# Differential attention in one float32 product instead of rounded halves

## The chip, the cores and the metric

The kernel runs on one core of a Trainium2 chip. The metric is the device time of one execution in microseconds (us), from start to end; of several executions the median is given. The core has a matrix engine (TensorE, "PE" in the profile, with its weight loads listed apart as "PEld"), a vector engine (VectorE, "DVE"), a scalar engine (ScalarE, "ACT"), a general one (GpSimd, "POOL") and a queue that issues transfers (SyncE, "SP"). Each works through its own list of instructions in a fixed order and waits at semaphores for the others.

## The reference, cut to what matters

One layer of an encoder on 1024 tokens of width 1024: a half-step feed-forward block, then two attention mixers side by side, a gated sum, and a second half-step feed-forward block. The change concerns the second mixer, the differential attention, with 4 heads, two maps of 64 for queries and keys per head, and values of width 128 (128 queries at a time, keys in chunks of 64 up to the query's own):

```python
sc = jnp.einsum('bqhrd,bkhrd->bhrqk', qblk, k).astype(jnp.float32) * scale
...
p = jax.nn.softmax(sc, axis=-1)
attn = p[:, :, 0] - lam * p[:, :, 1]
return jnp.einsum('bhqk,bkhe->bqhe', attn.astype(v.dtype), v)
...
o = rms_norm(o, subln_g) * (1.0 - lambda_init)
```

## The kernel before, in words

Matrix products run on a rounded 32-bit format (float32r) and recover the lost bits by halves: a number is split into its rounded value "hi" and the rest "lo". `split` does this with one ACT cast (line 97) and one DVE subtraction (line 102). A large product is then three products, hi by hi, lo by hi and hi by lo (lines 128 to 130).

The stages follow each other: first feed-forward block; its output projection; the mixer's input projections (queries, keys, gates, and the values by `project_v`, once for each mixer, branch `br` 0 for the band attention "A" and 1 for the differential attention "B"); the attention jobs; the gated output; the second feed-forward block. Projections go to DRAM and come back by `load_qkv` head by head.

`project_v` hands each finished 128x2x256 block to its `sink`. For B it splits two row blocks of 128 tokens into tiles `vo` of 512 columns, in which a head's 128 hi columns stand beside its 128 lo columns, and stores them to DRAM (`v`).

The attention stage runs a list of jobs: 32 for A (4 pairs of heads by 4 double blocks by 2 heads), then 32 for B (4 heads by 8 query blocks of 128). A job is a generator with stages, and `run` interleaves up to five of them, so that one job's scores are computed beside an older one's products. A B job i of a head (i = 0 to 7, key width (i+1)*128):

- scores `sc` (lines 779, 780: `qs` by `ks` and by the exchanged `kl`) for both maps; DVE adds the bias `nb` (787), ACT takes the exponential (789); DVE combines both maps into one `pm` (922 to 927).
- `transpose_p` turns `pm` in blocks of 128 on PE into `pt` (795), up to four blocks a tile, and splits it into `whi` and `wlo` (97, 102).
- for each of the i+1 key blocks two products into `pv`: `whi` by the 256 columns of `vt`, hi and lo (943), and `wlo` by its 128 hi columns (944). That makes 144 blocks over the 32 jobs.
- ACT scales both column halves of `pv` into `o1` and `o2` (946, 948), POOL adds them (949), DVE takes the mean square (952), POOL the power (`r`, 139) and the diagonal tile `dg` (955), PE the product `try` of `o1` and `dg` (958; both operands are plain float32), and ACT and DVE split it into `y` (99, 104).

Beside the jobs, one step of a filler (`branch_a`) is emitted every two B jobs: it loads a gate tile `gl`, makes 12 products `pb` of 512 columns, multiplies them (DVE, 892) and stores them to `ta` (893). Four times it also loads weights `wa`. The weights `raw` of `w_branch_b` and further `gl` come at the end.

The tiles `qs`, `ks`, `kl`, `vt`, `y`, `nb` share one pool of 14 buffers (`big`); `pv` and `pb` share two PSUM buffers. All loads and stores named here are issued by SP in one fixed order. That order, and the order on each engine, is set at build time by a scheduler that works on its own estimate of the times, so a change of one instruction can move others.

Of the kernel before, what the change touches and what calls it, by code (L numbers as in the profile page):

```python
# [54 lines left out]
def hybrid_layer_kernel(ctx, tc, x, ffn1_norm, ffn1_w_in, ffn1_w_out, mix_norm, w_mix_in,  # L55
# [516 lines left out]
    v_d = drams(2, [S, 2 * HALF], "v", F32R)  # L572
# [67 lines left out]
    with tc.tile_pool(name="ps1", bufs=1, space=PSUM) as ps:  # L640
# [24 lines left out]
        def project_v(br, c0):  # L665
# [6 lines left out]
            def make_sink(a):  # L672
                def sink(th, blk, ap):
                    for s in range(2):
                        o = sb.tile([P, HALF], F32R, tag="f", bufs=TF, name="vo")
                        if br == 0:
                            hi = bass.AP(o.tensor, o.offset, [o.ap[0], [256, 2], [192, 2], [1, 64]])
                            lo = bass.AP(o.tensor, o[:, 64:65].offset, [o.ap[0], [256, 2], [64, 2], [1, 64]])
                            src = ap[:, s, :].rearrange("p (a b d) -> p a b d", a=2, b=2)
                        else:  # L680
                            hi, lo = (o.rearrange("p (h c d) -> p h c d", h=2, c=2)[:, :, c, :] for c in range(2))
                            src = ap[:, s, :].rearrange("p (h d) -> p h d", h=2)
                        split(src, hi, lo)
                        t = 4 * th + 2 * a + s
                        move(nc.sync, v_d[br][t * P:(t + 1) * P, blk * HALF:(blk + 1) * HALF], o)
                return sink
# [63 lines left out]
    with tc.tile_pool(name="ps2", bufs=1, space=PSUM) as ps:  # L750
# [6 lines left out]
        def load_qkv(n, parts=1):  # L757
# [8 lines left out]
            vt = big([P, NT, 256], "vt")  # L766
            move(nc.sync, vt, v_d[n // 4].rearrange("(t p) c -> p t c", p=P)[:, :, (n % 4) * 256:(n % 4 + 1) * 256])
            return qs, ks, kl, vt

        def scores(qkv, h, i, k0, w):  # L770

            qs, ks, kl, _ = qkv
# [18 lines left out]
        def transpose_p(blocks):  # L791
# [4 lines left out]
            return split_units(pt[:, :len(blocks), :].rearrange("p b q -> p (b q)"))  # L796
# [22 lines left out]
        def jobs_a(pr):  # L819
            ctx_ = {}  # L820

            def job(sb_, h):
                if not ctx_:
                    ctx_["qkv"] = load_qkv(pr)
                    ctx_["y"] = big([P, 2, S], "y")
# [4 lines left out]
                qkv, y, nb = (ctx_[n] for n in ("qkv", "y", "nb"))  # L830
                vt = qkv[3]
# [65 lines left out]
        def jobs_b(hb, filler):  # L897
            ctx_ = {}

            def job(i):  # L900
                if not ctx_:
# [3 lines left out]
                    if hb % 2 == 0:  # L905
                        nbs.append(big([P, 2, S], "nb", F32))
                        for hh in range(2):
                            bias_rows(nbs[-1][:, hh, :], diag_b, hb + hh, EB, WB)
                    ctx_["nb"] = nbs[-1][:, hb % 2, :]
# [146 lines left out]
```

## Time and profile before

| | before |
|---|---|
| median of 3 executions | 2154.29 us (2150.46 to 2155.05) |
| span of the profiled execution | 2151.1 us |
| PE busy | 2080.7 us (97%) |
| DVE busy | 1442.3 us (67%) |
| ACT busy | 980.2 us (46%) |
| POOL busy | 181.4 us (8%) |
| moved by DMA | 333.55 MB |

For the profiled execution the profile gives the span from its first to its last instruction, and no time beside it. In the profile "busy" counts an instruction from its start to its end; matmuls overlap, and their ends are modelled, so the pace of PE is read from the distance between starts, and not from durations. A group's row gives the number of instructions, their busy time and mean duration in ns, and behind the bar the idle time of the engine just before them with what ended it. PEclk is the granted clock of TensorE as a share of full speed. One 128-column float32 matmul of the program appears as two weight loads and two matmuls in the trace (`try`: 32 in the program, 64 records).

### The profile page before, as it was taken

Reading aid. Unit: us, or ns where it says so; the run is one execution under the profiler, and the core shown is the slowest. Engines: PE = TensorE matmul, PEld = TensorE weight load, DVE = VectorE, ACT = ScalarE, POOL = GpSimd, SP = SyncE. Lnnn points to the kernel's source line nnn. Section 1 sums busy time; section 2 is a strip of 40 time slices with the busy share of each in tenths; the row PEclk is TensorE's granted clock in tenths of the full one; section 3 lists DMA queues with packets and bytes.
Section 4 is the critical chain, followed back from the end, with each engine's and each line's share of the span. In section 5 each row is a group of like instructions: output and inputs, shape, how many; then the busy total and the mean of one; then the engine's idle time right before and its main releaser. Section 6 shows DMA issues by size and latency. Waiting matters only on the chain.

```text
span 2151.1 us, 29100 instructions
## 1 busy us (share of the span) xinstructions
PE 2080.7 (97%) x10073; PEld 1738.7 (81%) x10073; DVE 1442.3 (67%) x2650; ACT 980.2 (46%) x1919; POOL 181.4 (8%) x282
## 2 busy tenths in 40 slices
PE   6999999999999999999999988999999999999997
PEld 5788888888888788899788877788788888888886
DVE  7666566677577756566488977558766656658566
ACT  5433333334446544444498665146433333334444
POOL 2120000000001000000066233001000000000001
PEclk9999999999999999999999999999999999999999
DMA  6653333294445544553683364634543333366334
GB/s 194 173 169 111 95 96 120 93 327 143 117 128 162 168 142 164 198 196 136 230 275 105 136 211 133 233 119 151 172 156 95 111 96 95 114 237 228 98 117 158
DMA packets 277555, 333.55 MB, mean 155 GB/s; under 512 B 15404, under 2 KB 167996, under 8 KB 277408
## 3 DMA queue, kind: packets, MB, share of 16 engines
q1 hardware_dynamic: 276080, 327.94, 46.7%
q0 software_dynamic: 1184, 3.24, 0.6%
q8 instruction: 79, 1.29, 0.3%
q14 instruction: 68, 0.56, 0.1%
q10 hardware_dynamic: 144, 0.52, 0.1%
HBM read 226.45 MB, written 105.19 MB: 154 GB/s over the span
## 4 chain that ended last, share of the span: by engine, by line
PE 82%; DVE 6%; DMA 4%; ACT 3%; issue 2%; SPq 1%; POOL 0%; ACTq 0%; DVEq 0%; POOLq 0%
PE prod L128 18%; PE prod L129 18%; PE prod L130 18%; PE po L129 7%; PE po L128 7%; PE po L130 7%; DVE wlo L102 2%; PE pb L128 1%; PE pb L130 1%; PE pb L129 1%; ACT pm L789 1%; DMA raw<-in_ffn_w_in_dram 1%; ACT whi L97 1%; PE tr L205 1%; PE pt L795 1%
## 5 line engine op out<-in xcount | busy, mean ns | idle before, releaser
L129 PE MATMUL po<-wlo,whi 128*128 128x512 f32 x744 | 290.6, 391 | 2.2 <-DVE wlo L102 2.2
L130 PE MATMUL po<-whi,wlo 128*128 128x512 f32 x744 | 289.4, 389 | 0.0
L97 ACT CAST whi<-raw 128x512 fp32r<-128x512 f32 x200 | 124.3, 622 | 308.1 <-PE prod L129 238.3
L97 ACT CAST whi<-B 128x512 fp32r<-128x512 f32 x186 | 115.8, 623 | 272.0 <-PE po L129 265.4
L97 ACT CAST whi<-T 128x512 fp32r<-128x512 f32 x192 | 119.4, 622 | 244.2 <-PE prod L129 224.7
L102 DVE TENSOR_TENSOR wlo<-B,whi 128x512 fp32r<-128x512 f32 x186 | 128.0, 688 | 139.3 <-ACT whi L97 139.2
L113 DVE TENSOR_TENSOR c<-prod,c 128x512 f32<-128x512 f32 x190 | 131.1, 690 | 133.6 <-PE prod L130 121.1
L102 DVE TENSOR_TENSOR wlo<-raw,whi 128x512 fp32r<-128x512 f32 x200 | 137.0, 686 | 106.6 <-ACT whi L97 64.0
L128 PE MATMUL po<-whi 128*128 128x512 f32 x744 | 201.5, 390 | 0.0
L102 DVE TENSOR_TENSOR wlo<-T,whi 128x512 fp32r<-128x512 f32 x192 | 131.8, 687 | 92.1 <-ACT whi L97 90.8
L129 PEld LDWEIGHTS po<-wlo,whi 128*128 128x128 f32 x744 | 139.6, 188 | 33.7 <-DVE wlo L102 5.1
L139 POOL TENSOR_TENSOR r<-v,neg_half 128x1 f32<-128x1 f32 x64 | 49.7, 780 | 1383.0 <-DVE v L180 1264.7
L130 PEld LDWEIGHTS po<-whi,wlo 128*128 128x128 f32 x744 | 139.7, 188 | 28.7
L128 PEld LDWEIGHTS po<-whi 128*128 128x128 f32 x744 | 139.1, 188 | 28.8 <-ACT whi L97 0.2
L102 DVE TENSOR_TENSOR wlo<-N,whi 128x512 fp32r<-128x512 f32 x64 | 44.1, 689 | 113.6 <-PE prod L129 62.9
L102 DVE TENSOR_TENSOR wlo<-ha,whi 128x512 fp32r<-128x512 f32 x154 | 105.4, 684 | 9.0 <-ACT whi L97 9.0
L272 ACT COPY c<-prod 128x512 f32<-128x512 f32 x186 | 103.1, 586 | 11.2 <-DMA hA<-c 4.4
L97 ACT CAST whi<-ha 128x512 fp32r<-128x512 f32 x154 | 94.8, 615 | 16.9 <-PE prod L129 11.4
L789 ACT ACTIVATE pm<-pm,mn 128x640 f32<-128x640 f32 (+7 forms) x128 | 94.0, 736 | 11.8 <-DVE ri L924 6.1
L128 PE MATMUL prod<-S1h,whi 128*128 128x512 f32 x240 | 94.4, 393 | 2.4 <-ACT S1h L97 1.4
L787 DVE CUSTOM_DVE_ANT_0 pm<-sc,nb 128x640 f32<-128x640 f32 (+7 forms) x128 | 87.9, 698 | 11.4 <-PE sc L780 8.8
L128 PE MATMUL prod<-S2h,whi 128*128 128x512 f32 x240 | 94.0, 392 | 1.3 <-ACT whi L97 1.3
(237 smaller groups left out, 5338.9 us busy)
## 6 DMA issues: line engine op xcount, KB each, us to landing
raw<-in_ffn_w_in_dram SPq DMA_DIRECT2D x98, 512.0 KB, 4.3
raw<-in_w_mix_in_dram SPq DMA_DIRECT2D x47, 512.0 KB, 4.4
ha<-hS SPq DMA_DIRECT2D x88, 256.0 KB, 2.6
hA<-c SPq DMA_DIRECT2D x66, 256.0 KB, 4.2
ha<-hA SPq DMA_DIRECT2D x66, 256.0 KB, 2.7
B<-in_ffn_w_out_dram SPq DMA_DIRECT2D x12, 1024.0 KB, 10.2
hS<-hs SPq DMA_DIRECT2D x44, 256.0 KB, 2.7
hS<-c SPq DMA_DIRECT2D x44, 256.0 KB, 4.4
```

What stands on the lines that cost most here:

```text
L97: nc.scalar.copy(out=hi, in_=src)
L102: (nc.gpsimd if on_pool else nc.vector).tensor_tensor(out=lo, in0=src, in1=h, op=ALU.subtract)
L113: nc.vector.tensor_tensor(out=out_, in0=a, in1=b, op=op)
L128: nc.tensor.matmul(ps, a[0], b[0], start=first, stop=False, skip_group_check=shared)
L129: nc.tensor.matmul(ps, a[0], b[1], start=False, stop=False, skip_group_check=shared)
L130: nc.tensor.matmul(ps, a[1], b[0], start=False, stop=last, skip_group_check=shared)
L139: nc.gpsimd.tensor_tensor(out=r, in0=v, in1=neg_half, op=ALU.pow)
L205: nc.tensor.transpose(tr[:, k, :], rows[:, k * P:(k + 1) * P], ident)
L272: nc.scalar.copy(out=self.held[name], in_=p)
L787: nc.vector.tensor_tensor_reduce(out=d3, in0=sc, in1=nb.rearrange("p (n w) -> p n w", n=n), scale=1.0, scalar=3e38, op0=ALU.add, op1=ALU.m ...
L789: nc.scalar.activation(out=dst, in_=dst, func=AF.Exp, bias=mn, scale=-1.0, accum_out=rs)
L795: nc.tensor.transpose(pt[:, b, :], p, ident)
```

## The change

For B the values are stored once, as plain float32, directly from the block that the projection leaves (the last block of the two halves, which still lies in PSUM, is copied by ACT first). Two heads' values, 128 columns each, come in one tile `vt`, loaded with the bias tile of the same two heads; odd heads load no values. The transposed probabilities are copied once by ACT as plain float32 (`pT`) and not split. Each key block takes one plain float32 product of 128 columns in place of the two rounded ones, `pv` has 128 columns, and there is one scaling on ACT and no sum on POOL. A's values and jobs keep their form.

```diff
--- before.py
+++ after.py
@@ -569,7 +569,8 @@
     q_d = drams(8, [P, 2, S], "q", F32R)
     k_d = drams(8, [P, 2, S], "k", F32R)
     kx_d = drams(8, [P, 2, S], "kx", F32R)
-    v_d = drams(2, [S, 2 * HALF], "v", F32R)
+    va_d = dram.tile([S, 2 * HALF], F32R, name="va")
+    vb_d = dram.tile([S, HALF], F32, name="vb")
     g_d = drams(2 * KT, [P, S], "g")
     ta_d = drams(KT, [P, S], "ta")
     diag_a = dram.tile([A_HEADS, SKEW, EA], F32, name="diag_a")
@@ -671,18 +672,22 @@
 
             def make_sink(a):
                 def sink(th, blk, ap):
+                    t0 = 4 * th + 2 * a
+                    if br == 1:
+                        if (th, blk) == (1, 0):
+                            o = temp([P, 2, 256], "vo")
+                            nc.scalar.copy(out=o, in_=ap)
+                            ap = o
+                        nc.sync.dma_start(out=vb_d[t0 * P:(t0 + 2) * P, blk * 256:(blk + 1) * 256].rearrange(
+                            "(s p) c -> p s c", p=P), in_=ap)
+                        return
                     for s in range(2):
                         o = sb.tile([P, HALF], F32R, tag="f", bufs=TF, name="vo")
-                        if br == 0:
-                            hi = bass.AP(o.tensor, o.offset, [o.ap[0], [256, 2], [192, 2], [1, 64]])
-                            lo = bass.AP(o.tensor, o[:, 64:65].offset, [o.ap[0], [256, 2], [64, 2], [1, 64]])
-                            src = ap[:, s, :].rearrange("p (a b d) -> p a b d", a=2, b=2)
-                        else:
-                            hi, lo = (o.rearrange("p (h c d) -> p h c d", h=2, c=2)[:, :, c, :] for c in range(2))
-                            src = ap[:, s, :].rearrange("p (h d) -> p h d", h=2)
+                        hi = bass.AP(o.tensor, o.offset, [o.ap[0], [256, 2], [192, 2], [1, 64]])
+                        lo = bass.AP(o.tensor, o[:, 64:65].offset, [o.ap[0], [256, 2], [64, 2], [1, 64]])
+                        src = ap[:, s, :].rearrange("p (a b d) -> p a b d", a=2, b=2)
                         split(src, hi, lo)
-                        t = 4 * th + 2 * a + s
-                        move(nc.sync, v_d[br][t * P:(t + 1) * P, blk * HALF:(blk + 1) * HALF], o)
+                        move(nc.sync, va_d[(t0 + s) * P:(t0 + s + 1) * P, blk * HALF:(blk + 1) * HALF], o)
                 return sink
             ch = [Combine(ps, [P, 2, 256], make_sink(a)) for a in range(2)]
             for ms in ((0, 1), (2, 3), (4, 5), (6,)):
@@ -763,13 +768,17 @@
                 for dst, src in ((qs, q_d[n]), (ks, k_d[n]), (kl, kx_d[n])):
                     move(nc.sync, dst[:, :, c],
                          bass.AP(src.tensor, src.offset + c.start, [[S, P], [P * S, 2], [1, S // parts]]))
-            vt = big([P, NT, 256], "vt")
-            move(nc.sync, vt, v_d[n // 4].rearrange("(t p) c -> p t c", p=P)[:, :, (n % 4) * 256:(n % 4 + 1) * 256])
-            return qs, ks, kl, vt
+            return qs, ks, kl
+
+        def load_v(src, n, dtype):
+
+            vt = big([P, NT, 256], "vt", dtype)
+            move(nc.sync, vt, src.rearrange("(t p) c -> p t c", p=P)[:, :, n * 256:(n + 1) * 256])
+            return vt
 
         def scores(qkv, h, i, k0, w):
 
-            qs, ks, kl, _ = qkv
+            qs, ks, kl = qkv
             n = 1 if w <= HALF else 2
             wc = w // n
             sc = ps.tile([P, 2, HALF], F32, tag="sc", bufs=2, name="sc")
@@ -788,12 +797,17 @@
                                            scale=1.0, scalar=3e38, op0=ALU.add, op1=ALU.min, accum_out=mn)
             nc.scalar.activation(out=dst, in_=dst, func=AF.Exp, bias=mn, scale=-1.0, accum_out=rs)
 
-        def transpose_p(blocks):
+        def transpose_p(blocks, whole=False):
 
             pt = ps.tile([P, 4, P], F32, tag="pt", bufs=2, name="pt")
             for b, p in enumerate(blocks):
                 nc.tensor.transpose(pt[:, b, :], p, ident)
-            return split_units(pt[:, :len(blocks), :].rearrange("p b q -> p (b q)"))
+            src = pt[:, :len(blocks), :].rearrange("p b q -> p (b q)")
+            if not whole:
+                return split_units(src)
+            dst = sb.tile(list(src.shape), F32, tag="w", bufs=WU, name="pT")
+            nc.scalar.copy(out=dst, in_=src)
+            return dst
 
         def bias_rows(dst, diag, h, length, w):
 
@@ -822,13 +836,13 @@
             def job(sb_, h):
                 if not ctx_:
                     ctx_["qkv"] = load_qkv(pr)
+                    ctx_["vt"] = load_v(va_d, pr, F32R)
                     ctx_["y"] = big([P, 2, S], "y")
                     ys.append(ctx_["y"])
                     ctx_["nb"] = big([P, 2, S], "nb", F32)
                     for hh in range(2):
                         bias_rows(ctx_["nb"][:, hh, :WA], diag_a, 2 * pr + hh, EA, WA)
-                qkv, y, nb = (ctx_[n] for n in ("qkv", "y", "nb"))
-                vt = qkv[3]
+                qkv, vt, y, nb = (ctx_[n] for n in ("qkv", "vt", "y", "nb"))
                 i0, i1 = 2 * sb_, 2 * sb_ + 1
                 first = [max(0, i - 4) for i in (i0, i1)]
 
@@ -903,12 +917,12 @@
                     ctx_["y"] = big([P, 2, S], "y")
                     ys.append(ctx_["y"])
                     if hb % 2 == 0:
-                        nbs.append(big([P, 2, S], "nb", F32))
+                        nbs.append((big([P, 2, S], "nb", F32), load_v(vb_d, hb // 2, F32)))
                         for hh in range(2):
-                            bias_rows(nbs[-1][:, hh, :], diag_b, hb + hh, EB, WB)
-                    ctx_["nb"] = nbs[-1][:, hb % 2, :]
-                qkv, y, nb = (ctx_[n] for n in ("qkv", "y", "nb"))
-                vt = qkv[3]
+                            bias_rows(nbs[-1][0][:, hh, :], diag_b, hb + hh, EB, WB)
+                    ctx_["nb"] = nbs[-1][0][:, hb % 2, :]
+                    ctx_["vt"] = nbs[-1][1][:, :, (hb % 2) * P:(hb % 2 + 1) * P]
+                qkv, vt, y, nb = (ctx_[n] for n in ("qkv", "vt", "y", "nb"))
                 w = (i + 1) * P
                 pr, rs = [], []
                 for r in range(2):
@@ -930,23 +944,18 @@
                 yield
                 pts = []
                 for b0 in range(0, i + 1, 4):
-                    pts.append(transpose_p([pr[0][:, b * P:(b + 1) * P] for b in range(b0, min(b0 + 4, i + 1))]))
+                    pts.append(transpose_p([pr[0][:, b * P:(b + 1) * P] for b in range(b0, min(b0 + 4, i + 1))], True))
                 due[0] += 0.5
                 while due[0] >= 1:
                     due[0] -= 1
                     next(filler, None)
                 yield
-                pv = ps.tile([P, 256], F32, tag="pv", bufs=2, name="pv")
+                pv = ps.tile([P, P], F32, tag="pv", bufs=2, name="pv")
                 for kb in range(i + 1):
-                    c = slice((kb % 4) * P, (kb % 4 + 1) * P)
-                    pt = pts[kb // 4]
-                    nc.tensor.matmul(pv, pt[0][:, c], vt[:, kb, :], start=kb == 0, stop=False)
-                    nc.tensor.matmul(pv[:, 0:P], pt[1][:, c], vt[:, kb, 0:P], start=False, stop=kb == i)
+                    nc.tensor.matmul(pv, pts[kb // 4][:, (kb % 4) * P:(kb % 4 + 1) * P], vt[:, kb, :],
+                                     start=kb == 0, stop=kb == i)
                 o1 = temp([P, P], "o1")
-                nc.scalar.activation(out=o1, in_=pv[:, P:], func=AF.Copy, scale=r1)
-                o2 = temp([P, P], "o2")
-                nc.scalar.activation(out=o2, in_=pv[:, :P], func=AF.Copy, scale=r1)
-                nc.gpsimd.tensor_tensor(out=o1, in0=o1, in1=o2, op=ALU.add)
+                nc.scalar.activation(out=o1, in_=pv, func=AF.Copy, scale=r1)
                 sq = temp([P, P], "sq")
                 v = small.tile([P, 1], F32, tag="v", name="v")
                 nc.vector.tensor_tensor_reduce(out=sq, in0=o1, in1=o1, scale=1.0 / P, scalar=EPS,
```

How the order moved, at three places. First PE, at the last two B jobs (in the changed kernel lines stand 9 to 14 lower; 955 is the new product, 804 the transposition, 967 the product `try`). Before:

```order
L944 MATMUL pv_13679<-vt_13021,wlo_13612 128x128
L795 MATMUL pt_13653<-ident_66,pm_13513 128x128 x4
L943 MATMUL pv_13710<-vt_13021,whi_13649 128x256
L958 MATMUL try_13706<-dg_13636,o1_13628 128x128
L944 MATMUL pv_13710<-vt_13021,wlo_13650 128x128
```

Now:

```order
L804 MATMUL pt_13277<-ident_66,pm_13171 128x128 x4
L955 MATMUL pv_13308<-vt_12245,pT_13255 128x128 x3
L804 MATMUL pt_13284<-ident_66,pm_13171 128x128 x4
L967 MATMUL try_13325<-dg_13269,o1_13264 128x128
L955 MATMUL pv_13329<-vt_12245,pT_13282 128x128 x4
L955 MATMUL pv_13329<-vt_12245,pT_13289 128x128 x4
```

The alternation of a 256-column and a 128-column product has become runs of up to eight float32 products, and `try` no longer stands inside a job's products.

Second SP, at the loads of the fourth B head (`q7`, `k7`, `kx7`). Before:

```order
L119 DMA wa_13270<-in_w_branch_a_dram 128x4x256
L119 DMA gl_12819<-g4_205 128x512
L124 DMA qs_13015<-q7_182 128x2x1024
L124 DMA ks_13016<-k7_190 128x2x1024
L124 DMA kl_13017<-kx7_198 128x2x1024
L124 DMA vt_13021<-v1_200 128x8x256
L893 DMA ta4_221<-gl_12819 128x512
```

Now:

```order
L119 DMA gl_12580<-g4_205 128x512
L119 DMA wa_12958<-in_w_branch_a_dram 128x4x256
L124 DMA qs_12747<-q7_182 128x2x1024
L124 DMA ks_12748<-k7_190 128x2x1024
L907 DMA ta4_221<-gl_12580 128x512
L119 DMA gl_12711<-g5_206 128x512
L124 DMA kl_12749<-kx7_198 128x2x1024
```

The gate tile `gl` now stands ahead of the weights `wa`, the load of values is gone, and a store `ta`, which waits for DVE, stands ahead of `kl`.

Third SP again, at the weights for the stage behind the attention. Before:

```order
L119 DMA raw_13755<-in_w_branch_b_dram 128x4x256
L119 DMA raw_13841<-in_w_branch_b_dram 128x4x256
L893 DMA ta6_223<-gl_13402 128x512
L119 DMA raw_13927<-in_w_branch_b_dram 128x4x256
L119 DMA raw_14013<-in_w_branch_b_dram 128x4x256
L119 DMA gl_13554<-g7_208 128x512
```

Now:

```order
L119 DMA gl_13208<-g7_208 128x512
L907 DMA ta7_224<-gl_13208 128x512
L119 DMA raw_13363<-in_w_branch_b_dram 128x4x256
L119 DMA raw_13449<-in_w_branch_b_dram 128x4x256
L119 DMA raw_13535<-in_w_branch_b_dram 128x4x256
L119 DMA raw_13621<-in_w_branch_b_dram 128x4x256
L119 DMA gl_13291<-g7_208 128x512
```

The filler's last but one `gl` now stands ahead of the four weight loads, its last one behind them.

## The prediction

> **What bounds the kernel now.** I read the engines' shares on the page first, then a table of stretches, to find the stage that the change touches and whether it has anything to win:
>
> ```profile
> PE 2080.7 (97%) x10073; PEld 1738.7 (81%) x10073; DVE 1442.3 (67%) x2650; ACT 980.2 (46%) x1919; POOL 181.4 (8%) x282
> ```
>
> ```profile
> core 0: us, PE busy (x) PEld busy (x) DVE busy (x) ACT busy (x) POOL busy (x), PEclk, DMA share, GB/s
> 900.00:1060.00 160.00, 160.00 (x1007) 145.49 (x1007) 95.99 (x162) 69.30 (x132) 0.00 (x0) 1.00 0.49 171
> 1188.00:1355.00 167.00, 146.37 (x861) 126.17 (x860) 131.98 (x406) 101.83 (x274) 55.59 (x100) 0.97 0.51 172
> ```
>
> PE carries the kernel. The first row is the stretch with the value projections: PE has no idle time there, so what DVE, ACT and the store queue are spared in it moves no end. The second row is the B jobs: 167.0 us, PE busy 146.4, so 20.6 us are idle, and the clock of 0.97 shows more time lost behind pauses. DVE works 132.0 us of it. This stage is half bound by PE and half by chains across the engines; all that can be won lies in the 20.6 us, in the clock and in PE's own work. The waits of PE in this stage, the third view, say which chains:
>
> ```profile
> PE try L958 <- POOL dg L955: 4.6, 4, 2.2
> PE sc L779 <- DVE mn L787: 3.3, 5, 1.7
> PE pv L943 <- DVE gl L892: 2.8, 1, 2.8
> PE pv L943 <- ACT o L948: 2.3, 4, 1.0
> PE pt L795 <- DVE wlo L102: 1.1, 2, 0.8
> PE sc L780 <- DMA kl<-kx: 1.0, 1, 1.0
> PE try L958 <- DVE wlo L102: 0.8, 2, 0.4
> ```
>
> The columns are total us, times and the longest. Four of these rows end on instructions that the change removes or on chains that run through them (`wlo`, `o` of line 948, and `dg`, which comes after the sum on POOL); three hang on loads or on scores.
>
> **PE's own work.** Before, a key block costs a 256-column and a 128-column float32r product; now one float32 product of 128 columns. The trace has such a product already: `try`. I look at where it stands in a dense row of products and count from start to start:
>
> ```profile
> 1302.88 0.38 PE L958 MATMUL try<-dg,o 128*128 128x128 f32 x2
> 1303.02 0.31 PE L944 MATMUL pv<-vt,wlo 128*128 128x128 f32 x1
> 1303.16 0.33 PE L943 MATMUL pv<-vt,whi 128*128 128x256 f32 x1
> 1303.33 0.22 PE L944 MATMUL pv<-vt,wlo 128*128 128x128 f32 x1
> 1303.39 0.33 PE L943 MATMUL pv<-vt,whi 128*128 128x256 f32 x1
> ```
>
> From `pv` at 1303.16 to `pv` at 1303.39 a key block takes 0.23 us, of which the product of line 944 is 0.06 (1303.33 to 1303.39). From `try` at 1302.88 to 1303.16 are 0.28 us with one product of line 944 in them: the float32 product takes 0.22, as two passes. The weight loads set the old pace as well:
>
> ```profile
> 1302.77 0.30 PEld L958 LDWEIGHTS try<-dg,o 128*128 128x128 f32 x2
> 1302.99 0.19 PEld L944 LDWEIGHTS pv<-vt,wlo 128*128 128x128 f32 x1
> 1303.10 0.19 PEld L943 LDWEIGHTS pv<-vt,whi 128*128 128x128 f32 x1
> ```
>
> Two loads for `try` from 1302.77 to 1302.99 are 0.11 each, and 0.11 again to the next: the same price by weight loads, and two of them per block before and now. So 144 blocks x (0.23 - 0.22) = 1.4 us less. Bounds: an unhidden load in a run of float32 products would make 2 x (0.11 + 0.11) = 0.44 per block, 144 x 0.21 = 30 us more; and the loads fully hidden give 0.11 x 2 = 0.22, as taken. I take 0.22 because its row lies between neighbours of the same shape.
>
> The Trainium skill, page "FP8 and Floating Point Precision", section "TensorE Precision Notes", says that true FP32 takes four passes through the array, which speaks against the change. The trace has two records of weight load and matmul for one such product, so the four would be two records of two each. By four full pairs of 0.11 each a block would be 0.44 and the change a loss; by the row it is a draw.
>
> **What leaves the chains.** The next rows are groups of the B stage and, last, of the value projection and of plain copies:
>
> ```profile
> L102 DVE TENSOR_TENSOR wlo<-pt,whi 128x512 fp32r<-128x512 f32 (+3 forms) x48 | 26.3, 551 | 7.4 <-ACT whi L97 7.3
> L948 ACT ACTIVATE o<-pv,ri 128x128 f32<-128x128 f32 x32 | 11.7, 365 | 0.0
> L949 POOL TENSOR_TENSOR o<-o,o 128x128 f32<-128x128 f32 x32 | 14.7, 460 | 62.6 <-ACT o L948 62.6
> L97 ACT CAST whi<-pt 128x512 fp32r<-128x512 f32 x24 | 13.9, 584 | 16.5 <-PE pt L795 15.5 <-DVE gl L892 1.0
> L102 DVE TENSOR_TENSOR vo<-c,vo 128x256 fp32r<-128x256 f32 x24 | 9.5, 418 | 2.0 <-ACT vo L97 2.0
> L272 ACT COPY c<-prod 128x512 f32<-128x512 f32 x186 | 103.1, 586 | 11.2 <-DMA hA<-c 4.4
> ```
>
> - 48 subtractions `wlo`: 26.3 us of DVE's 132.0 go, and 0.55 us between `pt` and the first product of a key group.
> - The cast `whi` becomes a copy of the same size: 584 against 586 ns, nothing.
> - 32 scalings `o2` (11.7 us of ACT) and 32 sums (14.7 us of POOL) go: 0.37 + 0.46 = 0.83 us less from a job's last `pv` to its `dg`.
> - In the value projection 16 subtractions of 0.42 us and their casts go, two copies of 0.59 come, 16 stores become 8: nothing on the path, since PE's 160.00 of 160.00 covers them. If that cover were gone, they would still be a saving.
>
> PE's waits that end on these chains sum to 4.6 + 2.3 + 1.1 + 0.8 = 8.8 us. Bounds: nothing, if the next link is late instead, and 8.8. Four waits for `dg` cannot lose more than 4 x 0.83 = 3.3, four for `o` 4 x 0.37 = 1.5, the 1.9 for `wlo` go whole: 6.7. What is late next is `o1`, `r` and `dg`, which stay, and ACT's copy `pT`, which now alone releases the product. As PE that starts earlier also meets the next wait earlier, I take two thirds: 4.4 us.
>
> **Loads.** Two heads in four load 1 MB less, and the order of SP changes. These are issues with the median time to landing, and two places in SP's list:
>
> ```profile
> kl<-kx SPq DMA_DIRECT2D x8, 1024.0 KB, 9.6
> vt<-v SPq DMA_DIRECT2D x8, 1024.0 KB, 12.8
> ```
>
> ```profile
> 1279.61 0.38 SPq L119 DMA_DIRECT2D wa<-in_w_branch_a_dram  x1
> 1280.10 0.45 SPq L119 DMA_DIRECT2D gl<-g  x1
> ...
> 1325.73 3.10 SPq L119 DMA_DIRECT2D raw<-in_w_branch_b_dram  x2
> 1328.89 0.72 SPq L119 DMA_DIRECT2D gl<-g  x1
> ```
>
> ```profile
> 1250.00:1255.00 5.00, 3.27 (x26) 3.01 (x25) 2.42 (x12) 2.80 (x10) 0.45 (x1) 0.96 0.79 192
> 1280.00:1285.00 5.00, 3.50 (x21) 2.82 (x20) 4.18 (x12) 3.70 (x8) 1.87 (x4) 1.00 0.83 276
> 1285.00:1290.00 5.00, 5.00 (x20) 4.08 (x19) 2.92 (x10) 2.86 (x7) 1.61 (x2) 0.66 1.01 400
> 1330.00:1335.00 5.00, 2.62 (x18) 2.16 (x18) 2.58 (x10) 2.04 (x7) 2.71 (x4) 1.00 0.64 196
> ```
>
> At 1280 `gl` was issued behind `wa`, with the head's loads right behind it: PE loses 1.5 us of 5, and then 0.34 of 5, 1.7 us, to the clock. Now `gl` stands ahead of `wa`: that clock loss goes, 1.7 us. At 1330 PE loses 2.4 us to a `gl` behind the weights `raw`; the last but one `gl` is now ahead of them, the last one still behind, so I count 1.0 of the 2.8 us wait. The wait for `kl`, 1.0, I halve: its head loads 3 MB instead of 4, but `ks` and `kl` now stand behind a store `ta`, which waits for a product on DVE. Behind that store, should DVE be late, `ks`, `kl` and the next `gl` queue, and PE waits for `kl`. At 1250 the third head waits for its bias tile; it still loads 5 MB, so that stays. Sum 1.0 + 0.5 = 1.5 us; bounds nothing (or a wait for `kl` of a few us more) and 1.0 + 2.8.
>
> **Sum.** 1.4 (PE) + 4.4 (chains) + 1.5 (loads) + 1.7 (clock) = 9.0 us less, to be taken from a span of 2151.1; the median 2154.3 stands 3.2 above that span, and I take the difference from it: 2145.3, rounded to 2145. Two results of this kernel closer than about 0.2% (4.3 us) can't be told apart, since three executions before spread over 4.6.
>
> **The rivals.**
>
> - *No change that can be measured.* DVE's relief only uncovers the next wait. For it: PE's order is fixed, the largest single wait for scores (1.7, behind the bias tile's load) stays, and a shorter `pv` only brings that wait sooner. Against: DVE works 132.0 of 167 us, and 26.3 of it goes. It leaves the 1.4 and a part of the chains, up to 4: 2150 to 2153.
> - *Much faster.* With a fifth of DVE's work gone PE never waits in the stage: all 20.6 us and the 1.4 go, 2132. Against: loads and the end of the last job, whose `r` and `dg` nothing covers, remain.
> - *Slower: float32 products in runs don't keep the pace of a single one.* `try` stands between float32r products; eight float32 ones in a row are shown nowhere. At 0.44 a block the time is 2154.3 - 7.6 (the other gains) + 30 = 2177. Those 7.6 us over 144 blocks are 0.05 each, so it breaks even at 0.28 a block, and from 0.31 on (4.3 us more over 144) it is measurably slower. For it: the second load is hidden only by the pass before it. Against: it was hidden in `try`, 0.22 for both. Four passes, as the Trainium skill has it on the page named above, at the price of four loads would give this same time.
>
> **How the numbers follow.** Forecast 0.58 (2140 to 2149), much faster 0.11, no measurable change 0.20, slower 0.11. Faster by over 0.2% is 0.58 + 0.11 = 0.69, within 0.2% 0.20, slower 0.11. The range goes from 2132, where no wait is left, to 2157, which takes in the no-change case with a wait for `kl` of some us; it leaves out the slow case and a little more.
>
> **What would show it.** Right: the product's starts in the dense rows 0.22 to 0.23 apart; `wlo` of `pt`, line 948 and 949 gone; DVE near 106 us in the B stage and PE's idle time there down from 20.6 to about 14; a granted clock of 1.00 at the fourth head's begin; the stretch to 1060 unchanged. Wrong: starts at 0.3 or more, or new waits of scores for `ks` or `kl` at the second and fourth head.

## The result, and the profile after

The changed kernel took 2135.39 us (median of 4, 2132.98 to 2136.99) beside 2154.32 us for the kernel before (4, 2150.46 to 2155.05): a ratio of 0.9916, 95% interval 0.9902 to 0.9931, 18.9 us less. The forecast was 9 us less, 2145, with a range from 2132 to 2157. Run again beside the kernel before on another chip, it was 17.0 us faster (2135.6 for 2152.65).

The first line of the page after, and then the table of stretches of after and of before. The columns of the tables are those shown in the prediction: length, busy time (and instructions) of PE, PEld, DVE, ACT and POOL, PEclk, DMA share, GB/s. The second row of each table is the B stage, cut at the first product `pv` of the first B head and at the first `pb` of the next stage:

```profile
PE 2074.2 (97%) x10073; PEld 1735.9 (81%) x10073; DVE 1416.0 (66%) x2586; ACT 969.7 (45%) x1873; POOL 160.1 (8%) x250
```

```profile
900.00:1060.00 160.00, 160.00 (x1008) 145.52 (x1008) 90.13 (x146) 64.97 (x118) 0.00 (x0) 1.00 0.46 157
1190.00:1336.50 146.50, 136.08 (x853) 121.28 (x852) 110.07 (x356) 93.45 (x240) 34.93 (x68) 0.98 0.51 173
```

```profile
1188.50:1353.00 164.50, 143.90 (x852) 124.37 (x851) 131.51 (x404) 101.36 (x272) 55.59 (x100) 0.97 0.50 170
```

In the two profiled executions the whole span falls by 15.9 us, from 2151.1 to 2135.2. Everything comes from this stage: 164.5 us before, 146.5 after. PE's idle time in it falls from 164.5 - 143.9 = 20.6 to 146.5 - 136.1 = 10.4 us, and PE's busy time falls by 7.8. The stage begins 1.5 us later, and what follows it takes 798.1 us before and 798.7 after. The stretch with the value projections stays at 160.00 of 160.00.

PE's waits in the stage after (total us, times, longest):

```profile
PE sc L788 <- DVE mn L796: 4.5, 4, 2.9
PE try L967 <- POOL dg L964: 1.8, 1, 1.8
PE try L967 <- ACT pT L809: 1.4, 3, 0.9
PE pb L128 <- DVE y L104: 0.8, 1, 0.8
PE sc L788 <- DMA ks<-k: 0.8, 1, 0.8
```

The waits of products for `o2` and `gl` and those for the probabilities' `wlo` are gone, and three of the four for `dg`. The bias add (`mn`) grew from 3.3 to 4.5: 2.9 of it at one place, the third head's bias tile.

The pace of the new product in dense rows of after (start, duration, and at the end the number of records; two for one 128-column float32 product):

```profile
1300.88 1.06 PE L955 MATMUL pv<-vt,pT 128*128 128x128 f32 x8
1301.77 0.39 PE L967 MATMUL try<-dg,o 128*128 128x128 f32 x2
...
1331.17 1.95 PE L955 MATMUL pv<-vt,pT 128*128 128x128 f32 x16
1332.95 0.39 PE L967 MATMUL try<-dg,o 128*128 128x128 f32 x2
```

Four blocks take 1301.77 - 1300.88 = 0.89 us and eight take 1332.95 - 1331.17 = 1.78, both 0.2225 per block. The product runs at the price of `try`, in rows as well as singly.

To see where PE's busy time went, I summed over the stage the distance from each matmul's start to the next one's, as far as the duration of its record reaches:

| from start to start, in the stage | before, us | after, us |
|---|---|---|
| products `pv`, 144 blocks | 26.8 + 13.1 = 39.9 | 33.0 |
| per block | 0.277 | 0.229 |
| `pb` | 45.2 | 42.0 |
| scores `sc` | 36.0 | 37.0 |
| transpositions `pt` | 14.8 | 15.9 |
| `try` | 7.9 | 8.0 |
| `pv`, `pt` and `try` together, time at half clock counted half | 61.4 | 54.6 |

The old pair of products cost 0.277 us a block over the stage, and not the 0.23 of its dense row. The product of line 944 has 0.06 between starts in the dense row and 13.1 / 144 = 0.091 on average. These means are not the products' own price: they also hold time of the neighbours on PE, short waits and stretches in which the clock was granted by half (the experiment without the subtractions takes them apart). The last row counts the neighbours in and the half clock out. By it, the 18.0 us are 10.2 us of PE's idle time, 1.7 us of clock and 6.8 us of products, transpositions and `try`; scores and `pb` give 0.7 us back.

### The profile page after: what moved, and what is told of

Its sections match the earlier page's. It is cut to its first block, busy times and chain, and to the rows that moved or that the text cites. A ratio compares the mean times of both kernels' runs of the same rounds, so it can differ in the third digit from the quotient of the medians.

```text
span 2135.2 us, 28919 instructions
## 1 busy us (share of the span) xinstructions
PE 2074.2 (97%) x10073; PEld 1735.9 (81%) x10073; DVE 1416.0 (66%) x2586; ACT 969.7 (45%) x1873; POOL 160.1 (8%) x250
## 4 chain that ended last, share of the span: by engine, by line
PE 84%; DVE 6%; ACT 4%; issue 3%; DMA 3%; POOL 0%; SPq 0%; ACTq 0%; DVEq 0%; POOLq 0%
PE prod L128 19%; PE prod L129 19%; PE prod L130 19%; PE po L129 7%; PE po L130 6%; PE po L128 6%; DVE wlo L102 2%; ACT pm L798 1%; PE pb L128 1%; PE pb L129 1%; PE pb L130 1%; PE tr L205 1%; ACT whi L97 1%; PE pv L955 1%; PE sc L788 1%
## 5 line engine op out<-in xcount | busy, mean ns | idle before, releaser
L139 POOL TENSOR_TENSOR r<-v,neg_half 128x1 f32<-128x1 f32 x64 | 43.7, 687 | 1449.4 <-DVE v L180 1268.8
L97 ACT CAST whi<-ha 128x512 fp32r<-128x512 f32 x154 | 94.8, 616 | 16.9 <-PE prod L129 11.4
```

The source lines that it names most:

```text
L97: nc.scalar.copy(out=hi, in_=src)
L139: nc.gpsimd.tensor_tensor(out=r, in0=v, in1=neg_half, op=ALU.pow)
```

## The experiments

All comparisons are with the kernel before, run on the same chip in the same group of runs: 2154.32 us beside the first row of the table; 2152.33 beside values per head, second scaling, unread subtraction and DVE step; 2151.41 beside the product alone, before without the subtractions and the work on constants; 2152.65 beside the rest. The ratios and their intervals are estimated from all runs. A stage time is that of the profiled run, between the same two places as above.

| kernel | us (median) | ratio to before, 95% | B stage, us | DVE busy in it, us |
|---|---|---|---|---|
| after | 2135.39 | 0.9916 [0.9902, 0.9931] | 146.5 | 110.1 |
| after, run again | 2135.6 | 0.9928 [0.9915, 0.994] | 146.3 | 110.1 |
| values per head | 2136.99 | 0.9929 [0.9916, 0.9943] | 146.6 | 109.4 |
| second scaling and sum | 2136.07 | 0.9929 [0.9916, 0.9941] | 147.7 | 109.5 |
| unread subtraction from `pt` | 2144.47 | 0.9964 [0.9952, 0.9977] | 155.0 | 130.7 |
| DVE step ahead of the product | 2145.71 | 0.9975 [0.9964, 0.9985] | 156.4 | 129.0 |
| product alone, the rest undone | 2143.10 | 0.9961 [0.9949, 0.9974] | 154.4 | 131.0 |
| before without the subtractions | 2137.33 | 0.9934 [0.9922, 0.9947] | 147.6 | 111.2 |
| DVE work on constants | 2142.44 | 0.9955 [0.9942, 0.9969] | 144.8 | 109.8 |
| DVE work on `pm` | 2132.12 | 0.9909 [0.9895, 0.9922] | 143.9 | 127.5 |
| DVE work on `pT` | 2134.11 | 0.9923 [0.9909, 0.9936] | 143.1 | 128.9 |
| values behind the bias tile | 2131.41 | 0.9904 [0.989, 0.9917] | 138.3 | 106.5 |

### Values loaded per head again

```diff
                     ctx_["qkv"] = load_qkv(4 + hb)
+                    ctx_["v2"] = load_v(vb_d, hb // 2, F32)
...
-                        nbs.append((big([P, 2, S], "nb", F32), load_v(vb_d, hb // 2, F32)))
+                        nbs.append(big([P, 2, S], "nb", F32))
...
-                    ctx_["vt"] = nbs[-1][1][:, :, (hb % 2) * P:(hb % 2 + 1) * P]
+                    ctx_["vt"] = ctx_["v2"][:, :, (hb % 2) * P:(hb % 2 + 1) * P]
```

> The changed kernel with one change taken back: each differential head loads a value tile of its own (1 MB, into its own of the 14 big buffers), as before the change, so odd heads load 4 MB again; products, copies and sums stay as changed. Theory 'chains and DVE' (what went from the way between transposition, product and sum, and from DVE): 2135 to 2138 us, within 0.15% of the changed kernel. Theory 'loads' (fewer megabytes and a free buffer let the heads begin on time): most of the 19 us comes back, 2145 us or more.

Measured 0.9929, stage 146.6 us. Two heads' values in one tile, and with it 1 MB less for every second head, are worth nothing that can be measured.

### The second scaling and the sum on POOL again

```diff
                 nc.scalar.activation(out=o1, in_=pv, func=AF.Copy, scale=r1)
+                o2 = temp([P, P], "o2")
+                nc.scalar.activation(out=o2, in_=pv, func=AF.Copy, scale=zero)
+                nc.gpsimd.tensor_tensor(out=o1, in0=o1, in1=o2, op=ALU.add)
...
```

(`zero` is a tile of one column, filled with zeros at the start of the kernel.)

> The changed kernel with the second scaling on ACT (by a tile of zeros) and the sum on POOL put back between the product and the mean square: 0.83 us longer from a job's product to its diagonal tile. Theory 'chains': 2138 to 2142 us, and waits of PE for the diagonal tile come back (1.8 us, once, in the changed kernel; 4.6, four times, before). Theories 'DVE load' and 'loads': 2135 to 2137 us.

Measured 2136.07 us, 0.9929, where 'chains' asked for 2138 to 2142. The waits for `dg` came back in part, 2.6 us in three places, and the profiled stage, 147.7 us, is 1.2 us longer than after's; the times don't show it. The 0.83 us that the change takes out of each job's way from `pv` to `dg` is worth nothing that can be measured: I take it that other jobs' products cover it.

### A DVE subtraction that nobody reads

```diff
             nc.scalar.copy(out=dst, in_=src)
+            dead = sb.tile(list(src.shape), F32, tag="w", bufs=WU, name="dead")
+            nc.vector.tensor_tensor(out=dead, in0=src, in1=dst, op=ALU.subtract)
             return dst
```

> The changed kernel with the 48 subtractions of the transposed probabilities put back on DVE, into a tile that nothing reads: DVE has its 26 us of work again, but no product waits for it. Theory 'chains': 2136 to 2140 us. Theory 'DVE load' (DVE's order and its share of 80% of the stage made PE late): 2143 to 2149 us. Theory 'loads': 2135.

Measured 2144.47 us, 0.9964: about half of the gain is lost, by work whose result nobody takes. PE's waits in this kernel's B stage:

```profile
PE pv L957 <- ACT pT L809: 9.7, 14, 2.4
PE pt L804 <- DVE y L104: 2.2, 5, 0.6
PE try L969 <- POOL dg L966: 1.6, 1, 1.6
PE sc L788 <- DVE mn L796: 1.0, 3, 0.5
PE pt L804 <- DVE dead L811: 0.9, 1, 0.9
```

The product waits 14 times for ACT's copy of the transposed block; in the changed kernel waits for this copy cost PE 1.4 us, named at `try`. Only 0.9 us of waiting ends on the dead operation itself.

### A DVE step between the copy and the product

```diff
             nc.scalar.copy(out=dst, in_=src)
-            return dst
+            dst2 = sb.tile(list(src.shape), F32, tag="w", bufs=WU, name="pT2")
+            nc.vector.tensor_tensor(out=dst2, in0=src, in1=dst, op=ALU.max)
+            return dst2
```

> The changed kernel with a DVE operation of the same size put back between ACT's copy and the product (the product reads what DVE writes, the greater of the transposed block and its copy, which are equal). Theory 'chains': 2143 to 2148 us, clearly above the run in which nothing reads DVE's result. Theory 'DVE load': the same time as that run within 2 us. The product's own start-to-start time in its dense rows stays 0.22 us; by 'chains' its mean over the stage rises above the 0.228 of the changed kernel.

Measured 0.9975, stage 156.4 us; on the path or beside it, a DVE operation that reads `pt` costs nearly the same (the two intervals overlap). PE waits here:

```profile
PE try L969 <- DVE ri L940: 4.3, 3, 3.3
PE sc L788 <- DVE mn L796: 3.1, 6, 1.0
PE try L969 <- POOL dg L966: 2.7, 2, 1.8
PE try L969 <- DVE ri L938: 2.6, 1, 2.6
PE pt L804 <- DVE pT L811: 1.7, 2, 1.2
PE try L969 <- DVE pT L811: 1.5, 3, 0.8
```

DVE's names are now on most of PE's waits. The products themselves stay at 0.110 us a record, 0.220 a block; their mean did not rise, as 'chains' had it, and the time is not clearly above that of the unread subtraction.

### The product alone, the rest undone

Values per head, the second scaling with its sum and the DVE step are all put back (the three edits above together). What stays of the change is the single float32 product and the value stores.

> The changed kernel with the value tile of each head, the DVE step between copy and product, and the second scaling and the sum all put back: what is left of the change is the single float32 product (and the stores of values). If the parts add up: 2136 + 9.7 + 1 + 0 = 2147 us. Theory 'DVE alone': 2152 us, as before the change. Theory 'DVE and product': 2145 to 2148 us.

Measured 2143.10 us, 0.9961, 8.3 us below before (interval 5.6 to 11.0): faster than each of the three forecasts, and 9 us faster than 'DVE alone', which falls. The stage, with `pv` at 0.112 us a record or 0.224 a block:

```profile
1190.30:1344.70 154.40, 137.58 (x850) 119.50 (x850) 131.01 (x402) 99.50 (x270) 53.48 (x100) 0.99 0.53 180
```

The 8.3 us are what the exchange of the product is worth with the rest undone, and not PE's own work alone. Of the 10.1 us that this stage is shorter than before, 3.8 are idle time (20.6 to 16.8), 3.4 the clock (one stretch at half clock in place of three) and 4.0 products, transpositions and `try` (61.4 to 57.4, half clock taken out); scores and `pb` take 1.1 more. By `pv` alone it would be 39.9 - 144 x 0.224 = 7.6 us, but the steps of transpositions and `try` grow from 22.7 to 25.5 us.

### Before, without the subtractions

```diff
+            if nolo:
+                src = pt[:, :len(blocks), :].rearrange("p b q -> p (b q)")
+                hi = unit(list(src.shape), "whi")
+                nc.scalar.copy(out=hi, in_=src)
+                return hi, hi
             return split_units(pt[:, :len(blocks), :].rearrange("p b q -> p (b q)"))
...
```

The kernel before, in which both products of B read the rounded half; the low half of the probabilities is left out.

> The kernel before without the 48 subtractions: both products read the rounded half, so the low half of the probabilities is left out; the 256-column and the 128-column product, the second scaling, the sum and the loads stay as before. Theory 'DVE alone': all of the gain, 2135 to 2138 us. Theory 'DVE and product': DVE's part only, 2141 to 2146 us, with the old pair of products still at more than 0.25 us a key block over the stage.

Measured 2137.33 us, 0.9934, 14.1 us below before, as 'DVE alone' had it here. Stage 147.6 us, with the old products, the old loads and the old scaling:

```profile
1189.80:1337.30 147.50, 135.22 (x852) 119.06 (x851) 111.18 (x356) 100.43 (x272) 54.34 (x100) 0.99 0.56 190
```

The old pair of products takes 0.177 + 0.066 = 0.243 us a block here, against 0.277 with the subtractions. It is tempting to call the difference waiting for the low half, but the trace of before says otherwise. There, the products that are later than the dense row lose 7.3 us between them (a few are sooner). Some 2.6 us of it are no loss: 31 products of line 944 stand directly behind a transposition or `try`, and the next `pv` follows after 0.143 us in place of 0.060 (the prediction's rows have one of each, at 1303.02 and 1303.33), but the step ahead of them is shorter by as much, about 0.03 us in place of 0.11. 1.0 us is half clock. About 3.5 us stand at 23 products behind which the next matmul starts within 0.3 us of the semaphore that it waits for: there a short wait can hide, since the duration of a matmul's record is modelled and overlaps the next one, and a wait inside it counts as busy. The low half ended 6 of these (0.9 us); the others ended with `mn`, `ri`, `dg`, `gl`, `y` and one `whi`. So products, transpositions and `try` have to be taken together, with the half clock taken out: 61.4 us before, 56.9 without the subtractions, 54.6 after. PE's idle time falls from 20.6 to 12.3 us by the subtractions alone, and what half clock adds to PE's busy time from 5.1 to 0.4.

The subtractions alone give 14, the product alone 8, the whole change 17.0 to 18.9: the two overlap, by 3.5 to 5.4 us. So neither 'DVE alone' nor 'DVE and product' held in both kernels. In which waits the two overlap is not shown.

### DVE load without a link: a miss, and two that hit the stage

The subtraction could cost by DVE's load, by DVE's waiting for ACT at a fixed place in its list, or by its reading of `pt`. The first try subtracted a constant tile from itself, 48 times.

```diff
             nc.scalar.copy(out=dst, in_=src)
+            n = src.shape[-1]
+            one = bass.AP(ident.tensor, ident.offset, [ident.ap[0], [0, n // P], [1, P]])
+            nc.vector.tensor_tensor(out=junk.bitcast(F32)[:, :n].rearrange("p (b q) -> p b q", q=P), in0=one, in1=one,
+                                    op=ALU.subtract)
```

> The changed kernel with 48 DVE operations of the subtractions' sizes that read and write constants and scratch only: DVE's load without any hold on the transposed block's PSUM buffer. Theory 'DVE load': 2142 to 2146 us, as in the run with unread subtractions (2144.5). Theory 'PSUM buffer' (there the transposed block stayed occupied until DVE had read it, and the next transposition waited): 2135 to 2139 us.

Measured 2142.44 us, 0.9955, inside the range of 'DVE load', but with a B stage of 144.8 us. The operations depend on nothing, and the scheduler put them hundreds of us earlier; the stretch from 690 to 770 us of this kernel and of after:

```profile
690.00:770.00 80.00, 73.26 (x346) 59.30 (x345) 71.94 (x126) 36.12 (x64) 0.00 (x0) 0.96 0.50 150
```

```profile
690.00:770.00 80.00, 77.85 (x379) 63.70 (x378) 55.90 (x88) 39.81 (x69) 0.00 (x0) 1.00 0.55 163
```

DVE does 38 instructions more there and PE 33 fewer, and the B stage begins 6.4 us later than in after (1196.4 for 1190.0). The 7 us lost say nothing about the B stage. The next two are tied to it by what they read: `pm`, which DVE itself made, and then ACT's copy `pT`.

```diff
             nc.scalar.copy(out=dst, in_=src)
+            n = src.shape[-1]
+            pm = bass.AP(blocks[0].tensor, blocks[0].offset, [blocks[0].ap[0], [1, n]])
+            nc.vector.tensor_tensor(out=junk.bitcast(F32)[:, :n], in0=pm, in1=pm, op=ALU.subtract)
             return dst
```

> The changed kernel with 48 extra DVE subtractions of the old sizes, anchored in the B stage: each reads the probabilities pm that DVE itself made, and writes a scratch tile that nobody reads. They wait for no other engine, hold no PSUM buffer and release nothing; DVE's load in the stage goes back to about 132 us. Theory 'DVE load' (DVE's work in front of the scores' and means' work is what cost time): 2143 to 2146, B stage 153 to 156 us, as with the unread subtractions from PSUM. Theory 'DVE waits for ACT in its fixed order' and theory 'the PSUM buffer pt is held until DVE has read it': 2135 to 2138, B stage 146 to 148.

```diff
             nc.scalar.copy(out=dst, in_=src)
+            nc.vector.tensor_tensor(out=junk.bitcast(F32)[:, :src.shape[-1]], in0=dst, in1=dst, op=ALU.subtract)
             return dst
```

> The changed kernel with 48 extra DVE subtractions that read only ACT's copy pT and write a scratch tile that nobody reads: each waits for ACT's copy at its place in DVE's list, but does not read the PSUM tile pt. Theory 'DVE load': 2143 to 2146, like the one that reads pm. Theory 'DVE waits for ACT in its fixed order': 2142 to 2146, while the one that reads pm stays at 2135 to 2138. Theory 'the PSUM buffer is held': 2135 to 2138, since pt comes free with ACT's copy; only reading pt from DVE then costs time.

The B stage of the two, and of the unread subtraction from `pt`:

```profile
1188.90:1332.80 143.90, 134.04 (x853) 118.59 (x852) 127.48 (x402) 93.57 (x240) 41.28 (x68) 1.00 0.52 176
```

```profile
1190.00:1333.10 143.10, 133.98 (x853) 118.44 (x852) 128.90 (x404) 92.56 (x240) 38.67 (x68) 1.00 0.53 176
```

```profile
1189.40:1344.40 155.00, 138.45 (x853) 119.78 (x852) 130.65 (x404) 93.49 (x240) 37.69 (x68) 0.99 0.48 164
```

All three have 48 subtractions more than after, of the same sizes; their group's rows:

```profile
L812 DVE TENSOR_TENSOR junk<-pm 128x512 f32<-128x512 f32 (+3 forms) x48 | 26.1, 544 | 0.1
```

```profile
L810 DVE TENSOR_TENSOR junk<-pT 128x512 f32<-128x512 f32 (+3 forms) x48 | 26.7, 556 | 3.1 <-ACT pT L809 2.7
```

```profile
L811 DVE TENSOR_TENSOR dead<-pt,pT 128x512 f32<-128x512 f32 (+3 forms) x48 | 25.8, 549 | 3.2 <-ACT pT L809 3.1
```

DVE works 127 to 131 us in all three, and in the last two it waits about 3 us for ACT's copy. Only the one that reads the PSUM tile `pt` is slow: 155.0 against 143.9 and 143.1 us. The other two measured 2132.12 and 2134.11 us, which is even below the 2135 to 2138 that the theories without load had. DVE's load and its place in line are out as causes. That ACT and DVE slow each other when both read `pt` is out too: ACT's copy takes 475 ns after the change, 474 with the subtraction from `pt` and 477 with the work on `pT`, and the subtractions take 544 to 556 ns in all three.

How the reading of `pt` becomes time is shown in part. There are two buffers `pt`, and from its first transposition to its last reader a buffer is held 1.37 us after the change (mean of 48), 1.31 with the work on `pT`, 2.65 with the subtraction from `pt`, and 2.56 before. But PE hardly waits for it: 0.9 us in the row above. What differs is PE's list. Between the last transposition of a group and the first product on it stand, in the median of the 48 groups, 14 matmul records in after, 12 with the work on `pm`, 13.5 with the work on `pT`, and 6.5 with the subtraction from `pt`. The product comes too close behind its transposition, and waits for ACT's copy, the 9.7 us above. Two more versions were built and their lists read, but they were not run: a subtraction that reads `pt` and writes the scratch tile gives 6 records, one that reads `pT` and writes a tile of the ring `w` gives 13. So the list follows the reading of `pt`, and not the tile `w` that the unread subtraction also takes. That the scheduler moves the transposition back because it holds the buffer for longer is my reading of this and is not shown. Before the change the list has 12.5 records and about 2.4 us there (2.1 to 2.2 after), and with the DVE step on the path 17.5 records and 3.4 us: with a second step on the path the loss takes another form, and the waits for `ri`, `mn` and `dg` above are where it shows. Which of the two forms has which share of the 14 us before is open.

### The values behind the bias tile

```diff
                     if hb % 2 == 0:
-                        nbs.append((big([P, 2, S], "nb", F32), load_v(vb_d, hb // 2, F32)))
+                        nb = big([P, 2, S], "nb", F32)
                         for hh in range(2):
-                            bias_rows(nbs[-1][0][:, hh, :], diag_b, hb + hh, EB, WB)
+                            bias_rows(nb[:, hh, :], diag_b, hb + hh, EB, WB)
+                        nbs.append((nb, load_v(vb_d, hb // 2, F32)))
```

This was run twice. At first:

> The changed kernel with the two heads' value tile loaded behind the bias tile instead of ahead of it. In the changed kernel PE waits 2.9 us in one piece for the third head's first scores, which wait for the bias tile. If that transfer is what the stage waits for there: 2131 to 2134 us. If the queries and keys come too late as well, or the scheduler's order takes it back: 2135 to 2138.

Measured 2131.08 us, 0.9906 [0.9892, 0.9919]. Then beside the changed kernel on one chip:

> The changed kernel itself, on the chip of the three other runs of this group, so that they can be compared with it directly. All theories: 2133 to 2137 us, ratio to before 0.990 to 0.993, B stage 146 to 147 us from the first product to the first product of the next stage.

> The changed kernel with one move: the two heads' values are loaded behind their bias tile instead of ahead of it, run on the chip of the changed kernel for a direct comparison. Theory 'the third head waits for its bias tile, and the values ahead of it are part of that wait': 2130 to 2133 against 2133 to 2137, 3 to 5 us less, the wait of scores for the bias add below 1 us. Rival, 'the gain seen earlier was the chip or one pause that came elsewhere': within 2 us of the changed kernel.

Measured 2131.41 (2129.75 to 2132.12) beside 2135.6 (2134.46 to 2138.89): 4.2 us less, and the two sets of runs don't touch. It beats both kernels. PE's waits in the stage, first of the changed kernel on this chip, then of this one:

```profile
PE sc L788 <- DVE mn L796: 5.1, 4, 3.5
PE try L967 <- POOL dg L964: 1.8, 1, 1.8
PE try L967 <- ACT pT L809: 1.5, 4, 0.8
```

```profile
PE try L968 <- ACT pT L809: 2.3, 5, 0.7
PE try L968 <- POOL dg L965: 1.8, 1, 1.8
PE pv L956 <- DVE gl L906: 1.0, 1, 1.0
```

PE's wait for the bias add falls from 5.1 to 0.2 us, and the stretches of half clock at 1209 and 1257 us are gone with it. The stage's 138.3 us are not to be compared with 146.3 whole: its first product stands 3.6 us later, so some of the work now comes ahead of the cut; the stage ends 4.5 us earlier (1329.8 for 1334.3). Of the 5.1 us, 1.5 stood at the second head's scores, whose bias tile is issued before the stage begins (at 1160 us in the changed kernel). The kernel with the work on `pm` gained 3.5 us against the changed one too (2130.98 to 2133.45, its runs don't touch those of after either), with nothing but DVE work added. So the new order on the engines can give this much by itself, and how much of the 4.2 is the bias tile's own stays open.

## Why the prediction was right or wrong

The time lies in the range, at its fast end, but outside of the 2140 to 2149 us to which I had given 0.58, and the gain is twice the forecast. So the mechanism is right in part only, and the range owes its hit to the room that I had left for the rival without waits.

- **The place and the sign** were right: the stretch to 1060 us kept its 160.00, all of the gain lies in the B stage, and the products for `wlo`, the second scaling and the sum are gone.
- **The pace of the new product** was right: 0.22 forecast, 0.2225 in rows of four and eight blocks. The rival by which a second weight load is not hidden falls. The Trainium skill, page "FP8 and Floating Point Precision", section "TensorE Precision Notes", says that true FP32 takes four passes; the trace shows two records of weight load and matmul per product, and at 0.44 a block the kernel would have been at 2177 us.
- **PE's own work, 1.4 us forecast.** Products, transpositions and `try` fell by 6.8 us (61.4 to 54.6, half clock taken out). 4.5 of them go with the subtractions alone, while the old pair stays (56.9); 2.3 remain for the new product in the place of the old pair, between two kernels without the subtractions (they differ in the second scaling and the loads as well). So the price from dense rows was nearly right for the exchange itself. What the sum lacked is the rest: no term stood for what hides in PE's busy time. Short waits are a part of it; PE's waits table does not show them, because a wait shorter than a record's modelled duration is not idle time.
- **The chains, 4.4 us forecast.** PE's idle time fell by 10.2 us in all, more than the 8.8 us of the waits that I had picked. This is the term that was mis-sized most. I had put most of it on the way from `pv` to `dg`, by the names at the ends of the waits (`dg`, `o`); that part, put back, cost nothing that can be measured. The part that I had valued by its 1.9 us of named waits, the subtraction, is worth 14 us by itself. Its stage is 16.9 us shorter (164.5 to 147.6): 8.3 of idle time, 4.5 at products, transpositions and `try` and 4.7 of half clock, less 0.6 at scores and `pb`. A wait for `dg` names the last link only. Without the subtractions, and with the sum on POOL still there, the waits for `dg` fell from 4.6 to 2.6 us; that the delay came from products that ran late is my reading of this.
- **DVE's relief.** DVE fell to 110.1 us, near the 106 forecast, and idle time to 10.4, below the 14 forecast. But the 26 us taken off DVE are worth nothing as load: put back as work that reads `pm`, the time does not rise (2132.12 for 2135.6). The "much faster" rival argued from this load, as did my case against "no change"; both leaned on the wrong quantity.
- **Loads, 1.5 us forecast.** The wait for `gl` at 1330 and the one for `kl` at the second head are gone from the list. One for `ks` of 0.8 us is new, at the third head (1248 us), where I had not looked for it. Loading values per head again costs nothing measurable, so the megabyte less in every second head is worth nothing that can be measured; the order of `gl` and `wa` was not tried apart.
- **The clock, 1.7 us forecast.** Stretches of 3.4 us at half clock stood at 1255, 1285, 1337 and 1354 us before, and stand at 1211, 1259 and 1337 after: one fewer, 1.7 us. The sum is as counted, but partly by luck. The fourth head's first scores, at 1287 us, run at full clock (first row), as forecast; the stretch at 1354 went too, and a new one came at the second head's scores, behind two waits of PE of 0.65 and 0.82 us (second row). Neither of the two was foreseen:

```profile
1286.00:1291.00 5.00, 4.76 (x31) 4.08 (x30) 4.16 (x12) 3.78 (x8) 0.95 (x2) 1.00 0.66 205
```

```profile
1208.00:1213.00 5.00, 3.54 (x21) 3.13 (x20) 4.43 (x16) 3.56 (x8) 0.71 (x2) 0.81 0.31 123
```

## What to carry to other kernels

Price the work that you remove by its best row for the exchange itself, and then look at its mean over the stage, from start to start: what lies between the two (here 0.05 us a block) can be hidden waits, half clock and time of the neighbours, so count the neighbours in before you call it a gain. Where a scheduler sets the order at build time, an operation of an engine that isn't the bottleneck can be costly for the PSUM buffer that it reads and the order that follows from it, and not for its time; give it back as pure load, tied to its place by what it reads, before you blame the load. Put each removed link back by itself: the wait that carries a link's name may be worth nothing.

## What the hardware showed that was not expected

- A 128-column float32 product costs no more than a 256-column and a 128-column float32r product on the same block: 0.2225 against 0.23 us in dense rows.
- 26 us more work on DVE in a stage of 146 us, where it then is busy 127.5 of 143.9 us, made nothing slower; the kernel came out 3.5 us faster, with another order on the engines and two stretches of half clock fewer (PEclk 1.00 in place of 0.98).
- Unused work alone moves this kernel both ways through the order that the scheduler gives it: from 3.5 us faster (work on `pm`) to about 7 us (work on constants) and 9 us (subtraction from `pt`) slower. The 3.5 us are nearly as much as the 4.3 us that a single comparison can tell.
- A 128-column float32r product directly behind a plain float32 matmul starts about 0.03 us after it, where the next float32 matmul starts after 0.11, and the product behind it then follows after 0.143 us and not after 0.060 (31 places in the B stage before): the price of such a neighbourhood can only be read over both steps.
